# Attention's small operations moved from VectorE to GpSimd, its reciprocals moved behind the next group's minima, and an early root in the last stage

## The chip, the cores and the metric

The kernel runs on one core of a Trainium2 chip. A core has five engines with a queue of instructions each, which run in order: TensorE (PE in the profile, its weight loads PEld), VectorE (DVE), ScalarE (ACT), GpSimd (POOL) and SyncE (SP, which only issues DMAs here). The metric is the device time of one execution in microseconds, as the median of three runs: 1259.7 us (1258.15 to 1260.27).

## What is computed

One decoder layer over 1024 tokens of width 1024, in float32. Two branches read the same normalised input: a state-space branch and an attention branch with 16 heads of 64. Their outputs are gated, merged, projected and normalised. Of the reference, what the change touches is the softmax of the attention and the last norm:

```python
# attention, in blocks of 128 queries; fcum is a running sum of gates
s = einsum('bhqd,bhkd->bhqk', q[blk], k[:q1]) * scale
s = s + fcum[q0:q1, None] - fcum[None, :q1]
s = where(kpos <= qpos, s, -inf)
o[blk] = einsum('bhqk,bhkd->bhqd', softmax(s), v[:q1])
...
# end of the layer
out = einsum('bld,de->ble', merged, w_out)
x = x + out * rsqrt(mean(out * out) + eps) * post_g
```

## The kernel before, in words

**TensorE's work.** Nearly all time of TensorE goes into large projections. Each pair of output units is computed as seven half-size block products (a scheme that saves one product in eight), and each float32 operand is split into a high and a low part, so that one product is 12 matmuls of 128 x 128 x 512. `Pair` holds such a pair, `Stream` the fixed order of all its products, `halves(n)` issues the next n half products. Splits of operands (`wop` for weights at L366 and L367, `x0` to `x6` for activations at L273 to L279) lie on ScalarE (the high part, a copy) and on VectorE (the low part, a subtraction). Results leave PSUM by ScalarE (L426, L437) and VectorE (L439 to L443).

**The stages.** A prologue normalises the input; then the state-space branch, the attention (about 676 to 1108 us in the profile) and the last stages run, each with products of the stream between their own matmuls. The order on TensorE is written out by hand. On the other engines a scheduler places instructions, but those wrapped in `pin` keep their order among each other, and a `high_priority` block goes first.

**The attention.** Eight pairs of heads (`hp`), six groups each (`g`), 48 in all, counted by `m`. A group is two query blocks against one half of the keys:

```python
GROUPS = [((7, 4), 1), ((7, 4), 0), ((6, 5), 1), ((6, 5), 0), ((3, 0), 0), ((2, 1), 0)]
```

Blocks 7 and 4 (part 0) and 6 and 5 (part 1) take two groups, one for each half of the keys; blocks 3, 0, 2 and 1 (part 2) need only the lower half. So a part ends with each group of odd `g`; `end(m)` names it. In a round of the loop over `m`:

- `scores` issues the score matmuls into four PSUM tiles named `s`. Scores come out negated. For each of the four a VectorE instruction adds the gate sums `fb` and the mask and takes the row minimum `nm` (L1571, with a short read of the accumulator behind it), and ScalarE makes the exponential into `ex` with its row sum `sm` (L1575).
- `weighted` issues the matmuls of the group before, transposed weights `p` times values, into `av`. `free` (L1530) takes `av` out of PSUM.
- For a part that ends here, `settle` compares the minima of its two halves: `nr` is the smaller one (L1476), `dd` the difference of each to it (L1478, one instruction for each half), and ScalarE turns `dd` into exponentials (L1479).
- `masks` lets GpSimd write masks for later groups (L1437 into `fb`, L1446 into a part of `ex`).
- `stream.halves` issues projections.
- `scale` then forms the factors of the part: `sm` times `dd` (L1490), the sum over the two halves (L1492), its reciprocal (L1493), and `ns`, which is `dd` times one half times the reciprocal (L1495, twice). A part 2 has one half only: reciprocal (L1486) and half of it (L1487). All of it is on VectorE, on 4 or 8 columns.
- `turned` transposes the group's weights on TensorE into PSUM tiles that share their four buffers with `s`. ScalarE (L1614) and, for one block in four in the first six pairs, VectorE (L1612) copies them out to `p`; only then is the tile free for new scores. In the middle of the transposes of the group behind a part's end, TensorE transposes `ns` too; `send` and `take` bring it through DRAM into a broadcast form `rb`, and `out` multiplies by it (L1536, L1542, L1544).

GpSimd also issues the DMAs that store `ya_dram`, `ga_dram`, `ms_dram`, `t_s` and `t_a`; such an issue waits in GpSimd's queue for its data.

**The last stage.** `outcome(i)` takes row block `i` of the result in two halves `ch`: ScalarE squares the half and sums it into `ssq` (L1147), GpSimd multiplies by the norm's weights (L1150), and `finish` takes the square root on ScalarE (L1161), its reciprocal on VectorE (L1162) and writes the output (L1164). The square root needs another table in ScalarE than the exponentials and tanh before it; the load of it (ACT_TABLE_LOAD) stands in front of the first root.

Of the kernel before, what the change touches and what calls it, by code (L numbers as in the profile page):

```python
# [12 lines left out]
ALU = mybir.AluOpType  # L13
# [73 lines left out]
def hybrid_layer(ctx: ExitStack, tc, a, out):  # L87
# [43 lines left out]
    def pin(op):  # L131
        return tc.keep_in_program_order(op)

    def small(name="th"):
        return gp.tile([P, HALF], F32, tag="th", name=name)
# [995 lines left out]
    def outcome(i):  # L1131

        o, g, xr, st = {}, {}, {}, {}

        def begin(ch):
            xr[ch] = wp.tile([P, KH, P], F32, tag="raw", bufs=6, name="xr").rearrange("p a b -> p (a b)")
            nc.sync.dma_start(xr[ch], a["x"][i * P : (i + 1) * P, half(ch)])

        def dst(ch):
            o[ch] = fin["pool"].tile([P, HALF], F32, tag="ot", bufs=5, name="ot")  # L1140
            return o[ch]

        def post(ch):
            if not st:
                st["ssq"] = fin["pool"].tile([P, 2], F32, tag="ssq", bufs=4, name="ssq")
            ssq = st["ssq"]
            nc.scalar.activation(small("sq").bitcast(BF16)[:, 0:HALF], o[ch], AF.Square, accum_out=ssq[:, ch : ch + 1])  # L1147

            g[ch] = small("g") if i >= 6 else o[ch]
            (nc.vector if i >= 6 else nc.gpsimd).tensor_tensor(g[ch], o[ch], fin["postg"][:, half(ch)], ALU.mult)  # L1150
            if i == NT - 1:
                nc.vector.tensor_scalar(ssq[:, 1:2], ssq[:, 1:2], 1.0 / D, 4.0 * EPS, ALU.mult, ALU.add)
                return
            if len(o) < 2:
                return
            r = ssq[:, 0:1]
            nc.vector.tensor_tensor(r, r, ssq[:, 1:2], ALU.add)
            finish(r, eps4)

        def finish(r, bias):  # L1160
            nc.scalar.activation(r, r, AF.Sqrt, bias=bias, scale=1.0 / D)  # L1161
            nc.vector.reciprocal(r, r)  # L1162
            for c in range(2):
                nc.vector.scalar_tensor_tensor(o[c], g[c], r, xr[c], ALU.mult, ALU.add)  # L1164
                (nc.sync, nc.scalar)[c].dma_start(out[i * P : (i + 1) * P, half(c)], o[c])

        def direct(ch, ps):
            dst(ch)
            g[ch] = small("g")
            r = st["ssq"][:, 0:1]  # L1170
            with tc.high_priority():
                nc.scalar.activation(small("sq").bitcast(BF16)[:, 0:HALF], ps, AF.Square, accum_out=r)
                nc.vector.scalar_tensor_tensor(
                    g[ch], ps, -1.0, fin["postg"][:, half(ch)], ALU.mult, ALU.mult
                )
                finish(r, st["ssq"][:, 1:2])

        if i == NT - 1:
            post.direct = direct

        return dst, post, begin
# [214 lines left out]
    with tc.tile_pool(name="att", bufs=1, reuse_waits="tile", side="right") as ap, tc.tile_pool(  # L1396
# [55 lines left out]
        class Heads:  # L1452
# [16 lines left out]
            def settle(self, n):  # L1469

                if n == 2:
                    return
                nr = ap.tile([P, 2, 2], F32, tag="nr", name="nr")
                dd = self.dd[n] = ap.tile([P, 2, 2, 2], F32, tag="dd", name="dd")
                nm = self.nm[n]
                nc.vector.tensor_tensor(nr, nm[:, :, 0], nm[:, :, 1], ALU.min)  # L1476
                for h in range(2):
                    nc.vector.tensor_tensor(dd[:, :, h], nr, nm[:, :, h], ALU.subtract)  # L1478
                nc.scalar.activation(dd, dd, AF.Exp)  # L1479

            def scale(self, n):

                sm = self.sm[n]
                ns = self.ns[n] = ap.tile([P, 2, 2, 2], F32, tag="ns", name="ns")
                if n == 2:
                    nc.vector.reciprocal(sm, sm)  # L1486
                    nc.vector.tensor_scalar(ns, sm, 0.5, None, ALU.mult)  # L1487
                    return
                dd = self.dd[n]
                nc.vector.tensor_tensor(sm, sm, dd, ALU.mult)  # L1490
                total = sm[:, :, 0]
                nc.vector.tensor_tensor(total, total, sm[:, :, 1], ALU.add)  # L1492
                nc.vector.reciprocal(total, total)  # L1493
                for h in range(2):
                    nc.vector.scalar_tensor_tensor(ns[:, :, h], dd[:, :, h], 0.5, total, ALU.mult, ALU.mult)  # L1495

            def turn(self, n, tp):

# [228 lines left out]
        def end(m):  # L1727

            hp, g = divmod(m, 6)
            if 0 <= hp < NK and g % 2:  # L1730
                yield heads[hp], g // 2
# [29 lines left out]
        for m in range(6 * NK + 1):  # L1761

            if m < 6 * NK:
                hp, g = divmod(m, 6)
                if not g:
                    heads[hp] = Heads(hp)
                for u in range(2):
                    scores(hp, g, u)
            for one in made:
                weighted(*one)  # L1770
            for hd, which in end(m - 1):
                hd.free(which)
            if m == 6 * NK:
                stream.release()
                heads[NK - 1].out(2)
                break
            for hd, which in end(m - 2):
                if hd.last and which and m < 6 * NK - 1:
                    hd.out(which)
            for fn in deferred:  # L1780
                fn()
            deferred.clear()
            stream.release()
            for hd, which in end(m):
                hd.settle(which)
            masks(m)
            ahead, behind = room(m)
            stream.halves(ahead)

            for hd, which in end(m):  # L1790
                hd.scale(which)
                hd.load_gates(which)
            if m == 6 * NK - 1:
                heads[hp].out(1)
                for fn in deferred:
                    fn()
                deferred.clear()
            loads(m)
            made = turned(hp, g, list(end(m - 1)))
            if g in (1, 3):  # L1800
                masked(hp, {1: 5, 3: 0}[g])
            for hd, which in end(m - 2):
                if not hd.last or not which:
                    hd.out(which)
            if m == 6 * NK - 1:
                tp = pp.tile([P, HALF], F32, tag="s", bufs=4, name="tp")
                heads[hp].turn(2, tp)
                heads[hp].send(2, tp)
            if m % 6 == 0:
                for fn in later:  # L1810
                    fn()
                later.clear()
            stream.hold()
            stream.halves(behind)
            for hd, which in end(m if m == 6 * NK - 1 else m - 1):
                hd.take(which)
# [59 lines left out]
```

## Time and profile before

| | |
|---|---|
| median of three runs | 1259.7 us |
| lowest and highest | 1258.15, 1260.27 us |
| the profiled execution | 1260.92 us, its span 1259.2 us |
| granted TensorE clock over it | 0.998 |
| the attention, span time | about 676 to 1108 us |
| last matmul begins | 1252.5 us |

The span runs from the first to the last instruction of the program; 1.7 us of the execution lie outside it. The page gives busy time by engine. A busy TensorE is not one at its peak, since matmuls overlap and their ends are modelled; so a late matmul is found by its start. A line of the timeline has the start in us from the span's start, the length, engine, source line, operation, the tiles written and read, the shapes and a count, and in brackets the idle time of the engine before it with what ended it. The wait lists say which instruction waited for which, with the total, the count and the longest.

### The profile page before, as it was taken

How to read it: one execution, taken by the hardware profiler on the slowest of the kernel's cores; microseconds unless marked ns; L12 is line 12 of the kernel's file. 1: busy time of each engine (PE TensorE's matmuls, PEld its weight loads, DVE VectorE, ACT ScalarE, POOL GpSimd, SP SyncE). 2: the span in 40 equal slices, each digit the busy share in tenths (PEclk: the TensorE clock that was granted, in tenths of full speed). 3: DMA queues.
4: the chain of work that ended last, by engine and by line, in shares of the span. 5: the costliest groups of instructions: out<-in, count | busy, mean ns of one | idle time of the engine just before them, and what ended most of it. 6: DMA issues, size and time to landing. Idle time of an engine off the chain costs nothing.

```text
span 1259.2 us, 20989 instructions
## 1 busy us (share of the span) xinstructions
PE 1238.8 (98%) x6920; PEld 992.1 (79%) x6920; DVE 1011.6 (80%) x1979; ACT 789.1 (63%) x1736; POOL 337.3 (27%) x384
## 2 busy tenths in 40 slices
PE   7999999999999999999999999999999999999997
PEld 5688888888888888888888777777777777788886
DVE  7898886888788977998776677767799767997975
ACT  7745665556655766567555666666686667843753
POOL 3000440013301241015111334333122332366062
PEclk9999999999999999999999999999999999999999
DMA  8143442655347443744465476666787667766932
GB/s 305 55 126 92 143 157 93 201 151 188 120 129 212 165 124 115 229 147 140 147 207 195 156 246 220 225 208 196 258 296 266 201 197 254 266 206 214 355 119 99
DMA packets 162476, 233.57 MB, mean 185 GB/s; under 512 B 15200, under 2 KB 73024, under 8 KB 162368
## 3 DMA queue, kind: packets, MB, share of 16 engines
q1 hardware_dynamic: 140400, 196.22, 48.9%
q10 hardware_dynamic: 16464, 17.93, 4.0%
q0 software_dynamic: 5504, 18.09, 3.7%
q8 instruction: 54, 0.88, 0.3%
q14 instruction: 54, 0.44, 0.1%
HBM read 162.99 MB, written 72.34 MB: 187 GB/s over the span
## 4 chain that ended last, share of the span: by engine, by line
PE 85%; ACT 5%; DVE 4%; DMA 4%; issue 1%; SPq 0%; DVEq 0%; ACTq 0%; POOL 0%
PE pb L126 37%; PE pc L126 21%; PE pd L126 7%; PE av L126 5%; PE pt L129 5%; PE s L126 5%; PE yps L126 2%; PE st L126 1%; ACT wop L366 1%; DMA xr<-in_x 1%; PE tr L129 1%; PE tr_v L129 1%; PE df L126 1%; DMA csb<-cs_dram 1%; DMA xt<-in_x 1%
## 5 line engine op out<-in xcount | busy, mean ns | idle before, releaser
L366 ACT ACTIVATE wop<-sum 128x512 fp32r<-128x512 f32 x180 | 112.3, 626 | 103.7 <-DVE sum L372 46.0
L367 DVE TENSOR_TENSOR wop<-sum,wop 128x512 fp32r<-128x512 f32 x180 | 135.4, 753 | 50.4 <-ACT wop L366 49.2
L1575 ACT ACTIVATE ex<-ex,nm 128x512 f32<-128x512 f32 (+1 forms) x192 | 116.4, 608 | 71.2 <-DVE nm L1571 69.4
L426 ACT ACTIVATE s<-pb 128x512 f32<-128x512 f32 x143 | 84.7, 593 | 90.0 <-PE pb L126 87.5
L126 PE MATMUL pb<-x0h,wop 128*128 128x512 f32 x384 | 131.5, 398 | 0.0
L126 PE MATMUL pc<-x3h,wop 128*128 128x512 f32 x384 | 129.8, 396 | 0.7 <-DVE ot L443 0.4
L126 PE MATMUL pc<-x2h,wop 128*128 128x512 f32 x384 | 130.0, 397 | 0.0
L126 PE MATMUL pb<-x4h,wop 128*128 128x512 f32 x384 | 129.2, 395 | 0.0
L126 PE MATMUL pb<-x5h,wop 128*128 128x512 f32 x376 | 126.9, 395 | 0.7 <-ACT s L426 0.7
L126 PE MATMUL pb<-x6h,wop 128*128 128x512 f32 x376 | 126.7, 395 | 0.7 <-ACT s L426 0.7
L367 DVE TENSOR_TENSOR wop<-raw,wop 128x512 fp32r<-128x512 f32 x144 | 106.6, 740 | 20.5 <-ACT wop L366 20.4
L1571 DVE CUSTOM_DVE_ANT_0 ex<-s,fb 128x512 f32<-128x512 f32 (+1 forms) x128 | 79.1, 652 | 30.0 <-PE s L126 24.5
L366 ACT ACTIVATE wop<-raw 128x512 fp32r<-128x512 f32 x144 | 89.8, 624 | 19.5 <-PE pd L126 12.2
L126 PE MATMUL pd<-x1h,wop 128*128 128x512 f32 x288 | 95.8, 392 | 0.0
L126 PEld LDWEIGHTS pc<-x3h,wop 128*128 128x128 f32 x384 | 72.1, 188 | 18.5 <-issue 2.4
L210 POOL TENSOR_TENSOR wd<-wd 128x256 f32<-128x256 f32 x32 | 31.6, 986 | 204.2 <-DMA wd<-in_wo 126.6
L126 PEld LDWEIGHTS pb<-x4h,wop 128*128 128x128 f32 x384 | 72.1, 188 | 17.3 <-issue 2.5
L126 PEld LDWEIGHTS pc<-x2h,wop 128*128 128x128 f32 x384 | 72.1, 188 | 17.1 <-issue 2.0
L126 PEld LDWEIGHTS pb<-x0h,wop 128*128 128x128 f32 x384 | 72.2, 188 | 16.0 <-issue 1.5
L126 PEld LDWEIGHTS pb<-x5h,wop 128*128 128x128 f32 x376 | 70.7, 188 | 17.7 <-issue 1.8
L126 PEld LDWEIGHTS pb<-x6h,wop 128*128 128x128 f32 x376 | 70.6, 188 | 17.1 <-issue 1.6
L126 PE MATMUL pb<-x4l,wop 128*128 128x512 f32 x192 | 75.0, 390 | 0.4 <-DVE x4l L1254 0.4
(315 smaller groups left out, 3038.7 us busy)
## 6 DMA issues: line engine op xcount, KB each, us to landing
raw<-in_wu SPq DMA_DIRECT2D x128, 256.0 KB
csb<-cs_dram SPq DMA_DIRECT2D x32, 256.0 KB
q<-q_dram SPq DMA_DIRECT2D x32, 256.0 KB
k<-k_dram SPq DMA_DIRECT2D x16, 512.0 KB
fb<-f_dram SPq DMA_DIRECT2D x16, 512.0 KB
rb<-st_dram SPq DMA_DIRECT2D x48, 128.0 KB
wd<-in_wo SPq DMA_DIRECT2D x40, 128.0 KB
xt<-in_x SPq DMA_DIRECT2D x8, 512.0 KB
```

The lines of the kernel that those rows point to most:

```text
L126: return tc.keep_in_program_order(nc.tensor.matmul(*args, **kw))
L129: return tc.keep_in_program_order(nc.tensor.transpose(out_, in_, idn))
L210: pin(nc.gpsimd.tensor_tensor(t[out_], t[a_], t[b_], ALU.subtract))
L366: nc.scalar.activation(op[:, 0], src, AF.Copy)
L367: self.low = nc.vector.tensor_tensor(op[:, 1], src, op[:, 0], ALU.subtract).ins
L426: self.kept = nc.scalar.activation(s, ps, AF.Copy).ins
L1571: nc.vector.tensor_tensor_reduce(o, s[e][:, 0:w], f[:, e], 1.0, 3.0e38, ALU.add, ALU.min, nm)
L1575: pin(nc.scalar.activation(o, o, AF.Exp, scale=-1.0, bias=nm, accum_out=hd.at(hd.sm, i, h, e)))
```

## The change

Four things are done, all in the attention but the last.

1. The two differences of `settle` become one instruction over both halves.
2. In `scale`, the product with `dd`, the sum over the halves and a doubling (in place of the factor one half) go to GpSimd. A part 2 has nothing there any more.
3. The reciprocal stays on VectorE, but moves to a new `factors`, called in the next round behind the scores of the next group, so it stands pinned behind that group's four minima. The last product, `ns`, goes to GpSimd, pinned too. The very last part stays on VectorE and where it was.
4. In the last stage, behind the first half of row block 1 on ScalarE, a square root of a single column is taken and thrown away.

```diff
             ssq = st["ssq"]
+            if (i, ch) == (1, 0):
+                pin(nc.scalar.activation(warm, epst, AF.Sqrt))
             nc.scalar.activation(small("sq").bitcast(BF16)[:, 0:HALF], o[ch], AF.Square, accum_out=ssq[:, ch : ch + 1])
...
                 nc.vector.tensor_tensor(nr, nm[:, :, 0], nm[:, :, 1], ALU.min)
-                for h in range(2):
-                    nc.vector.tensor_tensor(dd[:, :, h], nr, nm[:, :, h], ALU.subtract)
+                nc.vector.tensor_tensor(dd, nr.unsqueeze(2).to_broadcast([P, 2, 2, 2]), nm, ALU.subtract)
                 nc.scalar.activation(dd, dd, AF.Exp)
 
             def scale(self, n):
+
+                if n == 2:
+                    return
+                sm, dd = self.sm[n], self.dd[n]
+                nc.gpsimd.tensor_tensor(sm, sm, dd, ALU.mult)
+                total = sm[:, :, 0]
+                nc.gpsimd.tensor_tensor(total, sm[:, :, 1], total, ALU.add)
+                nc.gpsimd.tensor_tensor(total, total, total, ALU.add)
+
+            def factors(self, n):
 
                 sm = self.sm[n]
                 ns = self.ns[n] = ap.tile([P, 2, 2, 2], F32, tag="ns", name="ns")
                 if n == 2:
-                    nc.vector.reciprocal(sm, sm)
-                    nc.vector.tensor_scalar(ns, sm, 0.5, None, ALU.mult)
+                    if self.last:
+                        with tc.high_priority():
+                            nc.vector.reciprocal(sm, sm)
+                            nc.vector.tensor_scalar(ns, sm, 0.5, None, ALU.mult)
+                        return
+                    pin(nc.vector.reciprocal(sm, sm))
+                    pin(nc.gpsimd.tensor_scalar(ns, sm, 0.5, None, ALU.mult))
                     return
-                dd = self.dd[n]
-                nc.vector.tensor_tensor(sm, sm, dd, ALU.mult)
                 total = sm[:, :, 0]
-                nc.vector.tensor_tensor(total, total, sm[:, :, 1], ALU.add)
-                nc.vector.reciprocal(total, total)
-                for h in range(2):
-                    nc.vector.scalar_tensor_tensor(ns[:, :, h], dd[:, :, h], 0.5, total, ALU.mult, ALU.mult)
+                pin(nc.vector.reciprocal(total, total))
+                total = total.unsqueeze(2).to_broadcast([P, 2, 2, 2])
+                pin(nc.gpsimd.tensor_tensor(ns, self.dd[n], total, ALU.mult))
...
                 for u in range(2):
                     scores(hp, g, u)
+                for hd, which in end(m - 1):
+                    hd.factors(which)
             for one in made:
...
                 hd.scale(which)
+                if m == 6 * NK - 1:
+                    hd.factors(which)
                 hd.load_gates(which)
```

The order of TensorE's instructions stays as it was; on SyncE two loads change places. Three places show what moves. Lines of the changed kernel lie 2 to 13 further down than the same line before.

VectorE at the end of part 0 of the sixth head pair (953 to 962 us in the profile before): `ISA` is a minimum or the read of its accumulator, `x2l` a split of the stream, `th` and `wop` products and splits of it. Before:

```order
L1476 TENSOR_TENSOR nr<-nm 128x4
L1478 TENSOR_TENSOR dd<-nr,nm 128x2x2 x2
L439 TENSOR_TENSOR th<-pc,s 128x512
L277 SCALAR_TENSOR_TENSOR x2l<-x2l,x2h 128x512 x2
L1105 SCALAR_TENSOR_TENSOR th<-th 128x512
L367 TENSOR_TENSOR wop<-raw,wop 128x512
L1490 TENSOR_TENSOR sm<-sm,dd 128x8
L1612 COPY p<-pt 128x512
L1536 TENSOR_TENSOR zr<-o,rb 128x512
L1492 TENSOR_TENSOR sm<-sm 128x2x2
```

The same place in the changed kernel:

```order
L1478 TENSOR_TENSOR nr<-nm 128x4
L1479 TENSOR_TENSOR dd<-nr,nm 128x8
L439 TENSOR_TENSOR th<-pc,s 128x512
L277 SCALAR_TENSOR_TENSOR x2l<-x2l,x2h 128x512 x2
L1105 SCALAR_TENSOR_TENSOR th<-th 128x512
L367 TENSOR_TENSOR wop<-raw,wop 128x512
L1625 COPY p<-pt 128x512
L1549 TENSOR_TENSOR zr<-o,rb 128x512
```

The product and the sum are gone from here; the reciprocal of this part now stands behind the four minima that follow, and ahead of the `av` product of that round.

GpSimd at the same place: `ex<-fb,far` are masks, DMA rows are issues. Before:

```order
L1437 TENSOR_TENSOR fb<-fb,far 128x128 x2
L192 DMA t_a<-x 128x512
L192 DMA t_a<-y 128x512
L1106 DMA ms_dram<-th 128x512
L1446 TENSOR_TENSOR ex<-fb,far 128x256 x2
L1645 DMA ya_dram<-zr 128x512
L192 DMA t_a<-x 128x512
```

The same place in the changed kernel:

```order
L1439 TENSOR_TENSOR fb<-fb,far 128x128 x2
L192 DMA t_a<-x 128x512
L192 DMA t_a<-y 128x512
L1487 TENSOR_TENSOR sm<-sm,dd 128x8
L1489 TENSOR_TENSOR sm<-sm 128x2x2
L1490 TENSOR_TENSOR sm<-sm 128x2x2
L1448 TENSOR_TENSOR ex<-fb,far 128x256 x2
L1106 DMA ms_dram<-th 128x512
L1658 DMA ya_dram<-zr 128x512
L1508 TENSOR_TENSOR ns<-dd,sm 128x8
L192 DMA t_a<-x 128x512
```

Three small operations and later the factor come in, and the issue of `ms_dram` now stands behind the two masks and no longer ahead of them.

ScalarE in the last stage, where row block 1 begins (`ot` is a half of the result, `sq` its square). Before:

```order
L437 ACTIVATE ot<-pb 128x512
L366 ACTIVATE wop<-sum 128x512
L1147 ACTIVATE sq,ssq<-ot 128x512
L1161 ACT_TABLE_LOAD
L1161 ACTIVATE ssq<-ssq,eps_72 128x1
L366 ACTIVATE wop<-merged 128x512
```

The same place in the changed kernel:

```order
L437 ACTIVATE ot<-pb 128x512
L1148 ACT_TABLE_LOAD
L1148 ACTIVATE warm<-epst 128x1
L366 ACTIVATE wop<-sum 128x512
L1149 ACTIVATE sq,ssq<-ot 128x512
L1163 ACTIVATE ssq<-ssq,eps_72 128x1
L366 ACTIVATE wop<-merged 128x512
```

The load of the table stands two instructions earlier, in front of a split and not in front of the root.

## The prediction

> **What bounds the kernel now.** I read the busy times first, then the busy time by stretches of 40 us, then what TensorE waited for, and last the order of time around each wait. The first line of the page, with busy time, share of the span and instructions of each engine:
>
> ```profile
> PE 1238.8 (98%) x6920; PEld 992.1 (79%) x6920; DVE 1011.6 (80%) x1979; ACT 789.1 (63%) x1736; POOL 337.3 (27%) x384
> ```
>
> TensorE (PE) is the bound. VectorE (DVE) is 20% idle, so time taken off it counts only where TensorE waits for it. The busy time by stretches gives busy us of PE, PEld, DVE, ACT and POOL, then the granted clock, the DMA share and GB/s:
>
> ```profile
> 920.00:960.00 40.00, 37.94 (x250) 28.51 (x250) 39.78 (x90) 33.10 (x83) 12.88 (x22) 1.00 0.91 320
> 956.80:960.10 3.30, 1.83 (x16) 1.24 (x16) 3.30 (x6) 0.44 (x1) 1.85 (x3) 1.00 0.85 295
> 960.20:963.50 3.30, 3.30 (x17) 1.63 (x14) 1.71 (x12) 2.81 (x9) 0.56 (x1) 0.50 0.66 167
> ```
>
> From 920 to 960 us DVE has next to no idle time (39.78 of 40) and PE loses 2.06 us, more than in any other stretch of the attention. Directly behind, PE runs at half its clock (0.50). The waits of PE, with total us, times and the longest:
>
> ```profile
> PE s L126 <- DVE p L1612: 1.5, 1, 1.5
> PE s L126 <- ACT p L1614: 0.4, 1, 0.4
> PE pc L126 <- DVE ot L443: 0.4, 1, 0.4
> ```
>
> The first is the largest wait of PE in the attention or behind it, the third stands in the last stage. The same places in order of time (start, length, instruction, idle time before it):
>
> ```profile
> 922.79 1.95 PE L126 MATMUL av<-p,v 128*64 128x256 f32 x16
> 939.94 0.82 PE L126 MATMUL s<-k,q 64*128 64x128 f32 x6 [0.39 <-ACT p L1614]
> 957.00 0.90 PE L126 MATMUL s<-k,q 64*128 64x384 f32 x7
> 959.36 0.62 PE L126 MATMUL s<-k,q 64*128 64x256 f32 x5 [1.47 <-DVE p L1612]
> 959.91 3.48 PE L126 MATMUL av<-p,v 128*64 128x256 f32 x16
> ```
>
> PE stands 1.47 us for a copy of transposed weights, and the next sixteen matmuls take 3.48 us where sixteen of the same shape took 1.95 at 922.79: 1.5 us more. Why the copy was late, on DVE:
>
> ```profile
> 956.43 0.69 DVE L367 TENSOR_TENSOR wop<-raw,wop 128x512 fp32r<-128x512 f32 x1
> 957.04 1.67 DVE L1490 TENSOR_TENSOR sm<-sm,dd 128x8 f32<-128x8 f32 x1
> 958.63 0.68 DVE L1612 COPY p<-pt 128x512 f32<-128x512 f32 x1
> ```
>
> And on GpSimd (POOL) at the same time:
>
> ```profile
> 956.81 0.54 POOL L1106 DMA_DIRECT2D ms_dram<-th  x1 [6.57 <-DVE th L1105]
> 957.37 1.30 POOL L1446 TENSOR_TENSOR ex<-fb,far 128x256 f32<-128x256 f32 x2
> ```
>
> The copy queued behind one of the very instructions that the change moves, a product of 8 columns that took 1.67 us while POOL worked at the side and ended with it.
>
> **The change part by part.** *What leaves DVE.* The groups of the attention (count, busy us, mean ns, idle before):
>
> ```profile
> L1478 DVE TENSOR_TENSOR dd<-nr,nm 128x4 f32<-128x4 f32 x32 | 4.7, 189 | 0.5
> L1495 DVE SCALAR_TENSOR_TENSOR ns<-dd,sm 128x4 f32<-128x4 f32 x32 | 4.7, 188 | 0.3
> L1490 DVE TENSOR_TENSOR sm<-sm,dd 128x8 f32<-128x8 f32 x16 | 4.2, 262 | 7.0 <-ACT dd L1479 6.9
> L1492 DVE TENSOR_TENSOR sm<-sm 128x4 f32<-128x4 f32 x16 | 2.6, 162 | 0.4
> L1487 DVE TENSOR_SCALAR ns<-sm 128x8 f32<-128x8 f32 x8 | 2.2, 274 | 0.2
> ```
>
> Gone are 4.7 + 4.2 + 2.6 of the three groups in the middle, 7 of 8 of the last (1.9), and of the 32 differences one of each two (2.3): some 15 us in all, and 6.9 us of standing for the exponential. The reciprocals stay and move behind the next minima. Nearly all of this is worth nothing: PE waits for DVE by 1.5 us in the 430 us of the attention, so that is what a lighter DVE can give back, and what hangs on it.
>
> *The place at 957 us.* Without the product the copy can start where the product did, 957.04 instead of 958.63: 1.6 us earlier. Other edits in the full stretch cancel, some 0.2 us each: one product and one difference leave, one reciprocal comes in. What can eat the gain is POOL. The change puts three small additions and products on it, then, ahead of the DMA issue that used to hold them back, the two mask additions. The nearest rows for what POOL and DVE do to each other, first DVE:
>
> ```profile
> 793.08 1.10 DVE L1476 TENSOR_TENSOR nr<-nm 128x4 f32<-128x4 f32 x1
> ...
> 925.98 2.02 DVE L277 SCALAR_TENSOR_TENSOR x4l<-x4l,x4h 128x512 fp32r<-128x512 f32 x2
> ```
>
> Then POOL, with the spread of its narrowest operation last:
>
> ```profile
> 792.86 1.30 POOL L210 TENSOR_TENSOR x<-x,th 128x512 f32<-128x512 f32 x1 [7.76 <-DMA x<-ys_dram]
> ...
> 925.29 1.32 POOL L1446 TENSOR_TENSOR ex<-fb,far 128x256 f32<-128x256 f32 x2
> 926.57 1.72 POOL L1437 TENSOR_TENSOR fb<-fb,far 128x128 f32<-128x128 f32 x2
> L1437 POOL TENSOR_TENSOR fb<-fb,far x64: 420/432/977, 660.6 to 1089.0; 128x128 f32<-128x128 f32 x64
> ```
>
> At 793 a 4-column minimum stands until POOL's 1.30 us are over. At 926 two operations of each side take turns: POOL needs 1.72 us for what takes twice 0.43 alone. So in this kernel a DVE instruction on two SBUF tensors and a POOL one do not run together. [...]
>
> A small POOL operation is in no row. Below it is bounded by the 0.16 us that DVE needs for 4 columns (L1492), above by the 0.43 of 128 columns; I take 0.16, since the many times wider one costs only 0.43. Three of them ahead of the copy take 0.5 us from DVE, and the two mask additions 1.3 more if they too get in ahead. The copy then comes 1.6 us earlier (nothing in the way), 1.1 (the three small ones, by turns as at 926), or 0.2 later (all five first, as the product at 957 stood through both masks). I take 1.1, because the turns at 926 are the case with DVE work of the same size waiting.
>
> *The clock.* A wait of 1.47 − 1.1 = 0.4 us stays. The row at 939.94 has 0.39, and the stretch that holds it was granted 1.00. So I expect no half clock, and back come the 3.4 us at half speed: 1.7 us (1.5 by the two rows of sixteen matmuls, the rest on the matmul behind them). [...]
>
> *Reciprocals behind the next minima.* They no longer stand at the head of DVE's queue for sums that are not there. What is late next is the chain to the transposes of the factors on PE. The tightest of the 23, the last minimum on DVE:
>
> ```profile
> 1000.12 0.08 DVE L1571 DVE_READ_ACCUMULATOR2_ANT nm<- 128x1 f32 x1
> ```
>
> And PE:
>
> ```profile
> 1001.76 0.27 PE L129 MATMUL pt<-ident,ns 128*8 128x128 f32 x1
> ```
>
> From 1000.20 there are 1.56 us. A reciprocal (0.2), at most one DVE operation that holds POOL off (0.7) and the factor on POOL (0.16 to 0.43) end after 1.1 to 1.3 us. It fits, so nothing. POOL's masks come up to 2 us later, since they queue behind a factor that waits for the reciprocal; the minima that read them are a group, some 9 us, on.
>
> *The root of one column.* ScalarE (ACT) in the last stage:
>
> ```profile
> 1199.93 0.64 ACT L366 ACTIVATE wop<-sum 128x512 fp32r<-128x512 f32 x1 [1.47 <-DVE sum L372]
> 1201.19 1.28 ACT L1161 ACT_TABLE_LOAD   x1
> 1202.49 0.30 ACT L1161 ACTIVATE ssq<-ssq,eps 128x1 f32<-128x1 f32 x1
> ```
>
> DVE and then PE beside it:
>
> ```profile
> 1202.82 0.16 DVE L1162 RECIPROCAL ssq<-ssq 128x1 f32<-128x1 f32 x1 [1.45 <-ACT ssq L1161]
> 1202.89 0.67 DVE L443 TENSOR_TENSOR ot<-s,pc 128x512 f32<-128x512 f32 x1
> ...
> 1202.87 0.39 PE L126 MATMUL pb<-x4h,wop 128*128 128x512 f32 x1
> 1203.62 0.50 PE L126 MATMUL pc<-x3h,wop 128*128 128x512 f32 x1 [0.36 <-DVE ot L443]
> ```
>
> The 1.28 us load and a 0.30 root need 1.6 us and go into a gap of 1.47, so the next split starts 0.1 late at most. The square root, the reciprocal and the subtraction behind them come 1.2 us earlier. PE's matmuls of this size start 0.23 us apart; here it was 0.75, so 0.5 us of PE come back. Afterwards PE has work without a gap until the tail.
>
> Sum: 1.1 + 1.7 + 0.5 = 3.3 us. The profiled execution took 1260.92 us, which gives 1257.6. It lies 1.2 above the median of 1259.7, so the forecast for the median is 1256.4. A difference of 0.2%, 2.5 us, is about what a measurement of this kernel can tell from none; the runs of before spread over 2.1 us.
>
> **The rivals.** *POOL goes first.* [...] For it speaks the 1.67 us product, which stood through both masks; against it the turns at 926.
>
> *The clock falls anyway.* [...] Then 1.1 + 0.5 = 1.6, 1258.1. Against it: the half clock begins within 1 us of the wait's end, and nowhere else in the attention.
>
> *The factors come late.* [...] PE then stands at the transposes of the factors. By the same reading as at 1001.76 the seven third parts, the tightest, have margins of 1.6 to 3.3 us from the last minimum. At 3.0 us from minimum to factor, where this decides, they lose 3.8 us together, and the place at 957 gives nothing, since its three small operations cost as much: 1259.7 − 0.5 + 3.8 = 1263.0. For it speaks that no small POOL operation is in the trace; against it the 0.43 us of the wider one.
>
> **How the numbers follow.** The forecast has 0.47, the clock 0.18, POOL first 0.24, late factors 0.11. Faster by over 0.2% (below 1257.2) is the forecast and a sliver of the clock's case: 0.48. Slower is the last rival: 0.11. The same takes 0.41. The range reaches down to 1.6 + 1.7 + 0.5 and the 0.4 at 939.94, 4.2, and half the spread of the runs, 1.1: 1254.4. Up it takes POOL first with 0.8 of spread: 1260.2. The forecast's own range is 1255 to 1257.6.
>
> **What would show it.** Right: PE's list has no wait of over 0.6 us for a DVE copy, no stretch at 0.50 near 960, PE busy over 39.0 in the stretch from 920, no wait for ot in the last stage, and a table load that ends about when ACT's sum split can start. Wrong: a 128x8 operation on POOL over 0.5 us in the median, PE waiting at the transposes of ns, or the same 3 us given back at another full stretch of DVE.

## The result and the profile after

The changed kernel takes 1257.01 us in the median of 22 runs (1255.80 to 1258.01), the kernel before 1258.89 in as many runs beside them (1257.57 to 1262.59). The medians differ by 1.9 us. The ratio over the runs is 0.9983, with a 95% interval of 0.9976 to 0.9989: 2.1 us faster, between 1.4 and 3.0. The profiled execution of the changed kernel took 1256.17 us with a span of 1254.5, so the two profiled executions (1260.92 and 1256.17 us) are 4.75 us apart, more than twice what the medians differ by. Where the rest comes from is half of this study.

The busy line and the stretch from 920 us of the changed kernel, and of its list of what PE waits for the copies of p:

```profile
PE 1236.3 (99%) x6920; PEld 991.0 (79%) x6920; DVE 1003.6 (80%) x1892; ACT 789.4 (63%) x1737; POOL 358.9 (29%) x455
```

```profile
920.00:960.00 40.00, 39.03 (x262) 29.05 (x261) 39.50 (x93) 33.69 (x86) 15.35 (x27) 1.00 0.89 313
```

```profile
PE s L126 <- DVE p L1625: 0.4, 1, 0.4
...
PE s L126 <- ACT p L1627: 0.4, 1, 0.4
```

DVE is 8 us lighter, POOL 22 us heavier, and DVE is as full from 920 to 960 as it was (39.50 of 40). The wait of 1.5 us for p is gone, the wait for ot too. The 0.4 for a DVE copy of p is a wait at another place, 930.25, and a new one: neither profile of the kernel before has it. The place at 957 in the changed kernel, PE, then DVE, then POOL:

```profile
956.33 1.33 PE L126 MATMUL s<-k,q 64*128 64x384 f32 x12
957.59 1.95 PE L126 MATMUL av<-p,v 128*64 128x256 f32 x16
959.46 0.50 PE L126 MATMUL pb<-x5h,wop 128*128 128x512 f32 x1
```

```profile
953.88 1.29 DVE L277 SCALAR_TENSOR_TENSOR x2l<-x2l,x2h 128x512 fp32r<-128x512 f32 x2
955.09 0.68 DVE L1105 SCALAR_TENSOR_TENSOR th<-th 128x512 f32<-128x512 f32 x1
955.70 0.68 DVE L367 TENSOR_TENSOR wop<-raw,wop 128x512 fp32r<-128x512 f32 x1
956.30 0.68 DVE L1625 COPY p<-pt 128x512 f32<-128x512 f32 x1
```

```profile
954.15 0.48 POOL L1487 TENSOR_TENSOR sm<-sm,dd 128x8 f32<-128x8 f32 x1 [4.60 <-ACT dd L1480]
954.70 0.53 POOL L1489 TENSOR_TENSOR sm<-sm 128x4 f32<-128x4 f32 x1
955.31 0.52 POOL L1490 TENSOR_TENSOR sm<-sm 128x4 f32<-128x4 f32 x1
955.79 1.76 POOL L1448 TENSOR_TENSOR ex<-fb,far 128x256 f32<-128x256 f32 x2
```

The twelve score matmuls run through without a stop, and the sixteen behind them take 1.95 us at a granted clock of 1.00 (the stretch from 957.80 to 961.10). DVE's operations up to the copy keep their usual 0.6 to 0.7 us, one behind the other; it is the three small POOL operations that take 0.5 us each here. The masks still make DVE stand, but only the operation behind the copy (zr<-o,rb took 1.20 us, before 0.68), and PE does not wait for that one. The usual price of the small POOL operations is in the groups (minimum, median and maximum in ns):

```profile
L1487 POOL TENSOR_TENSOR sm<-sm,dd x16: 192/202/692, 687.3 to 1076.8; 128x8 f32<-128x8 f32 x16
L1508 POOL TENSOR_TENSOR ns<-dd,sm x16: 191/200/552, 696.4 to 1085.1; 128x8 f32<-128x8 f32 x16
L1503 POOL TENSOR_SCALAR ns<-sm x7: 227/228/452, 732.4 to 1047.0; 128x8 f32<-128x8 f32 x7
```

The last stage, ACT first, then PE:

```profile
1194.39 1.28 ACT L1148 ACT_TABLE_LOAD   x1
...
1195.96 0.63 ACT L366 ACTIVATE wop<-sum 128x512 fp32r<-128x512 f32 x1
...
1197.43 0.29 ACT L1163 ACTIVATE ssq<-ssq,eps 128x1 f32<-128x1 f32 x1 [0.23 <-DVE ssq L1159]
```

```profile
1198.78 0.39 PE L126 MATMUL pb<-x4h,wop 128*128 128x512 f32 x1
1199.01 0.39 PE L126 MATMUL pc<-x3h,wop 128*128 128x512 f32 x1
```

The load now stands where ACT had its gap of 1.47 us, the root takes 0.29 instead of standing behind 1.28, and the two matmuls are 0.23 us apart, where they were 0.75.

One number says most about each kernel below. From the first of the twelve score matmuls at that place to the matmul behind the sixteen products there are 28 matmuls in the same order in every kernel. In the kernel before they go from 957.00 to 963.32, 6.32 us; in the changed kernel from 956.33 to 959.46, 3.13. I call it the stretch of 28. The second number is the gap between the two matmuls of the last stage, 0.75 or 0.23.

### The profile page after: what moved, and what is told of

It reads as the page before. It is cut to its first block, busy times and chain, and to the rows that moved or that the text cites. A ratio compares the mean times of both kernels' runs of the same rounds, so it can differ in the third digit from the quotient of the medians.

```text
span 1254.5 us, 20953 instructions
## 1 busy us (share of the span) xinstructions
PE 1236.3 (99%) x6920; PEld 991.0 (79%) x6920; DVE 1003.6 (80%) x1892; ACT 789.4 (63%) x1737; POOL 358.9 (29%) x455
## 4 chain that ended last, share of the span: by engine, by line
PE 89%; ACT 4%; DVE 3%; DMA 3%; issue 1%; SPq 0%; DVEq 0%; ACTq 0%
PE pb L126 39%; PE pc L126 22%; PE pd L126 7%; PE av L126 5%; PE pt L129 5%; PE s L126 5%; PE yps L126 2%; PE st L126 1%; PE tr L129 1%; PE tr_v L129 1%; ACT wop L366 1%; PE df L126 1%; PE pv L126 1%; PE tr L126 0%; DMA raw<-in_wv 0%
## 5 line engine op out<-in xcount | busy, mean ns | idle before, releaser
L912 POOL TENSOR_TENSOR xe<-xdt,tend 128x256 f32<-128x256 f32 x28 | 26.2, 937 | 175.3 <-DVE xdt L875 170.3
```

What stands on the lines that cost most here:

```text
L912: nc.gpsimd.tensor_tensor(xe, s["xdt"], tend[:, c, hs].unsqueeze(2).to_broadcast([P, 4, 64]), ALU.mult)
```

## The experiments

Each was timed in five rounds beside the kernel before, on one of three chips. So medians of different rows do not compare as they stand: the kernel before took 1258.89 us beside the changed kernel, 1259.83 beside e1 to e4, 1260.26 beside e5 to e8 and 1260.17 beside e9 to e12. The intervals of most ratios are some 0.0009 to 0.0010 (1.2 us) to either side, so single ratios decide little between theories that differ by 1 us; the stretch of 28 and the gap are exact to some 0.05 us, but are those of one execution.

| kernel | median, us | ratio, 95% interval | stretch of 28, us | gap, us |
|---|---|---|---|---|
| before, first profile | | | 6.32 | 0.75 |
| changed | 1257.01 | 0.9983, 0.9976 to 0.9989 | 3.13 | 0.23 |
| e1 before again | 1259.85 | 1.0001, 0.9992 to 1.0010 | 4.79 | 0.75 |
| e2 root only | 1259.61 | 0.9994, 0.9985 to 1.0003 | 4.79 | 0.23 |
| e3 attention only | 1259.21 | 0.9989, 0.9979 to 0.9999 | 3.13 | 0.75 |
| e4 one place | 1258.94 | 0.9991, 0.9982 to 1.0000 | 3.22 | 0.74 |
| e5 masks behind copy | 1258.67 | 0.9986, 0.9977 to 0.9995 | 3.27 | 0.75 |
| e6 reciprocals in front | 1257.64 | 0.9978, 0.9970 to 0.9987 | 3.13 | 0.23 |
| e7 copy twice | 1258.52 | 0.9988, 0.9980 to 0.9997 | 3.89 | 0.23 |
| e8 copy three times | 1259.12 | 0.9991, 0.9982 to 1.0000 | 4.45 | 0.23 |
| e9 masks twice | 1263.36 | 1.0025, 1.0014 to 1.0037 | 7.64 | 0.74 |
| e10 small operations flood | 1275.68 | 1.0121, 1.0102 to 1.0141 | 3.16 | 0.23 |
| e11 masks behind copy, root | 1258.30 | 0.9984, 0.9973 to 0.9994 | 3.28 | 0.23 |
| e12 product behind copy | 1257.71 | 0.9979, 0.9969 to 0.9990 | 2.96 | 0.23 |

**The kernel before, again.** No edit.

> The kernel before, unchanged, profiled a second time and timed against itself. The profile of before showed a wait of 1.47 us for the copy of transposed weights at 957 us and 3.4 us at a granted clock of 0.50 behind it; against it the changed kernel gained 1.79 us in the wait and 1.5 us in the clock, 4.75 us over the whole span, while the medians of 22 runs each differ by 1.9. Theory A (the place is there in every execution, the half clock only in some, so that the first profile was an unlucky one): this profile shows a wait of 1.2 to 1.6 us at the same matmul and a granted clock near 1.00 behind it, and a span of about 1257. Rival B (wait and half clock are there every time, and the changed kernel gives something back in most executions): again 1.5 us and 0.50, span about 1259. Rival C (the wait itself comes and goes): under 0.6 us. Timed against itself: ratio 1.000.

The matmul at the place and the stretch that was at half clock in the first profile, in this second one:

```profile
959.35 0.62 PE L126 MATMUL s<-k,q 64*128 64x256 f32 x5 [1.47 <-DVE p L1612]
959.90 1.95 PE L126 MATMUL av<-p,v 128*64 128x256 f32 x16
```

```profile
960.20:963.50 3.30, 3.30 (x24) 2.26 (x21) 3.23 (x14) 2.85 (x10) 0.56 (x2) 1.00 0.50 154
```

The wait is there to the hundredth, 1.47 us, and the clock stays at 1.00. That is theory A: the wait is there again, the half clock is not. The span of 1257.7 is nearer to A's 1257 than to B's 1259.

**The early root alone.** The two lines of the change that stand in the last stage, in the kernel before.

```diff
+            if (i, ch) == (1, 0):
+                pin(nc.scalar.activation(warm, epst, AF.Sqrt))
```

> The kernel before with the early root alone. Theory: TensorE loses its 0.5 us wait for ot in the last stage, the ratio is 0.9996, 0.5 us faster; the wait at 957 us stays as it was. Rival (the table load of 1.28 us only moves and delays the splits behind it): 0.0 to +0.5 us, and a wait of TensorE of some 0.3 us for a weight split near 1199 us.

The gap falls from 0.75 to 0.23, so 0.52 us of PE come back, and no weight split delays PE instead. The ratio's middle, 0.9994, is 0.75 us; its interval includes none. The stretch of 28 is 4.79, wait and full clock, which makes the third profile with that wait and the second without a half clock.

**The attention's part alone.** The changed kernel without those two lines.

> The changed kernel without the early root, so the attention's part alone. Theory: it carries what is left of the 1.9 us between the medians, 1.4 us (ratio 0.9989), no wait for the copy near 957 us over 0.6 us and no half clock; TensorE waits 0.5 us for ot in the last stage as in the kernel before. Rival (the last stage carries most, the attention nothing): ratio 0.9998 or more.

The forecast of 0.9989 was met, and the stretch of 28 is the changed kernel's. The gap is back at 0.75. The span of this profile is 1259.5, above the kernel before's second one: PE waits 1.67 us for one matmul of an early stage, at 234.85 us, that the change does not touch. The mean granted clock of this execution is 0.999, as in the profiles of e1 and e2.

**One place.** Of the 16 groups of products only the one at 957 goes to GpSimd.

```diff
+        PLACE = (5, 0)
...
+                if (self.hp, n) == PLACE:
+                    sm, dd = self.sm[n], self.dd[n]
+                    nc.gpsimd.tensor_tensor(sm, sm, dd, ALU.mult)
...
```

> The kernel before with one of the attention's 16 groups of products changed, the one whose product took 1.67 us ahead of the copy at 957 us: its product, sum and doubling go to GpSimd, its reciprocal behind the next minima, its factors to GpSimd; its differences and all other groups stay on VectorE. Theory (the whole gain of the attention comes from this place): the same time as the attention's part alone, within 0.4 us, and a wait at 957 us under 0.6 us. Rival (the lighter VectorE of all 48 groups is what helps): at most a third of that gain, under 0.5 us.

The stretch of 28 is 3.22, 0.09 above the whole change, and the ratios are 0.9991 and 0.9989, each to some 0.001. The other 15 groups add no gain that can be seen.

**The masks behind the copy.** Nothing moves off VectorE. One column of p is copied on GpSimd ahead of the two mask additions, so that they can start only when the copy of p is done. If the two additions are why the product took 1.67 us, it takes 0.2 here, the copy comes 1.5 us earlier and PE's wait for it falls under 0.4 us.

```diff
             w = (i % 4 + 1) * P
+            if (hp, i) == (5, 5):
+                pin(nc.gpsimd.tensor_copy(seen, copies[31][:, 0, 1, 0:1]))
             for e in range(2):
```

> The kernel before with one more GpSimd instruction, a copy of one column of p, ahead of the two mask additions that ran beside the product of 1.67 us at 957 us. It reads the copy of transposed weights, so both mask additions start behind that copy; VectorE's order is that of before, word for word, and the product stays ahead of the copy. [...] Rival (the product was late or slow for its own inputs, or VectorE's queue is simply full there): product and wait as before, ratio 1.000.

DVE in this kernel, then POOL:

```profile
958.48 0.16 DVE L1494 TENSOR_TENSOR sm<-sm,dd 128x8 f32<-128x8 f32 x1
958.56 0.69 DVE L1617 COPY p<-pt 128x512 f32<-128x512 f32 x1
```

```profile
958.26 0.54 POOL L1106 DMA_DIRECT2D ms_dram<-th  x1 [6.57 <-DVE th L1105]
959.31 0.60 POOL L1448 COPY seen<-p 128x1 f32<-128x1 f32 x1 [0.51 <-PE s L126]
959.88 1.30 POOL L1450 TENSOR_TENSOR ex<-fb,far 128x256 f32<-128x256 f32 x2
```

The same product in the same place of the same queue, beside the same DMA issue, takes 0.16 us instead of 1.67, with both additions behind the copy. The mask additions were what held it. The wait at the place is gone, and the ratio of 0.9986 cannot be told from the 0.9989 of the attention's part.

**Reciprocals in front again.** The changed kernel with each reciprocal and factor product right behind its sum.

```diff
-                for hd, which in end(m - 1):
-                    hd.factors(which)
...
-                if m == 6 * NK - 1:
-                    hd.factors(which)
+                hd.factors(which)
```

> The changed kernel with each reciprocal and factor product right behind its sum again, so the reciprocals stand on VectorE ahead of the next group's minima; GpSimd keeps the small operations. Theory (VectorE then stands for sums that GpSimd has not finished, some 0.1 to 0.8 us each, and little of it reaches TensorE, which has slack in most groups): idle time of VectorE ahead of the 23 reciprocals 3 to 8 us in all against under 1 in the changed kernel, and a time 0.0 to 0.5 us above the changed kernel's (ratio 0.9983 to 0.9987). Rival (the move of the reciprocals is what carries the gain, since a standing VectorE delays its copies): at least 1 us back, ratio 0.9991 or more, with waits of TensorE for DVE p.

The group of the reciprocals, with the idle time of DVE ahead of them at the end:

```profile
L1506 DVE RECIPROCAL sm<-sm 128x4 f32<-128x4 f32 x16 | 2.8, 174 | 7.1 <-POOL sm L1490 7.0
```

DVE stands 7.0 us for GpSimd's sums, as the theory had it, and PE loses nothing by it: the stretch of 28 is 3.13 and the ratio 0.9978, if anything below the changed kernel's. Moving the reciprocals saves DVE 7 us that nobody waits for.

It even costs something, at 930 us. PE there in the changed kernel, with DVE and POOL ahead of it:

```profile
930.25 1.14 PE L126 MATMUL s<-k,q 64*128 64x384 f32 x11 [0.45 <-DVE p L1625]
```

```profile
926.99 2.03 DVE L279 TENSOR_TENSOR x1l<-x1l,x1h 128x512 fp32r<-128x512 f32 x2
928.95 0.92 DVE L367 TENSOR_TENSOR wop<-sum,wop 128x512 fp32r<-128x512 f32 x1
```

```profile
927.60 1.72 POOL L1439 TENSOR_TENSOR fb<-fb,far 128x128 f32<-128x128 f32 x2
```

The same operations with the reciprocals in front again:

```profile
928.71 1.28 DVE L279 TENSOR_TENSOR x1l<-x1l,x1h 128x512 fp32r<-128x512 f32 x2
929.91 0.68 DVE L367 TENSOR_TENSOR wop<-sum,wop 128x512 fp32r<-128x512 f32 x1
```

```profile
926.76 1.71 POOL L1439 TENSOR_TENSOR fb<-fb,far 128x128 f32<-128x128 f32 x2
```

In the changed kernel POOL waits for the reciprocal before the factor, so the masks behind the factor come later, by some 1.5 us. They now run beside DVE's splits x1l and wop (2.03 and 0.92 us instead of 1.28 and 0.68), and the copy of p stands behind these. The wait of 0.45 us is in the profiles of the changed kernel, e3, e7, e8 and e12; before, e1, e2, e4, e5, e6 and e11 have none there.

**The copy made twice, and three times.** The changed kernel with the copy of p at that place repeated (the edit for two copies; for three, `range(2 ...)`).

```diff
-                        nc.vector.tensor_copy(to, src)
+                        copies.append(p)
+                        one = nc.vector.tensor_copy(to, src)
+                        if len(copies) == 32:
+                            pin(one)
+                        for _ in range(1 if len(copies) == 32 else 0):
+                            pin(nc.vector.tensor_copy(to, src))
```

> The changed kernel with the copy of transposed weights at the place near 957 us made twice, and TensorE waits for the second; VectorE's order is the same otherwise. Its wait of 0.4 us there becomes 1.0. Theory (the clock falls behind a wait of about 1.5 us, in some executions): 0.6 us slower than the changed kernel, granted clock 1.00 behind the wait. Rival (any wait that is longer than the harmless 0.4 of the trace can halve the clock): 0.50 for some 3.4 us behind it, 2.3 us slower in the profile.

> The same with three copies; the third stands behind two of the next minima on VectorE, so the wait becomes about 0.4 + 2 x 0.6 + 2 x 0.6 = 2.8 us. Theory (the longer wait makes the fall of the clock the rule): 0.50 for 3.4 us or so behind it and 2.4 + 1.7 = 4.1 us slower than the changed kernel. [...]

Both expectations started from a wait of 0.4 that is not at this place (it is at 930.25). With two copies the wait is 0.57 and the stretch of 28 grows by 0.76; the ratio moves by 0.0005, as 0.6 us would. With three, PE's next score matmul does not wait for the third copy but for a minimum that comes before it, 1.02 us, and the stretch grows by 1.32, not 2.4. The clock is 1.00 in both. So waits of 0.57 and 1.02 us left the clock alone here, and the question of the longer wait was left to the next kernel.

**The masks made twice.** The kernel before, with the two mask additions that ran beside the product made over again.

```diff
-            for e in range(2):
+            for e in (0, 1, 0, 1) if (hp, i) == (5, 5) else (0, 1):
```

> The kernel before with the two mask additions that ran beside the product at 957 us made twice over, with the same operands, four in a row on GpSimd. VectorE's order up to the copy is that of before. Theory (the product stands until GpSimd's row of operations is over): the product takes 1.67 + 2 x 0.65 = 3.0 us, TensorE's wait there becomes 2.8 us instead of 1.5, the ratio 1.0010, and behind so long a wait the half clock comes in the profile too, 1.5 us more for such an execution. Rival (after two operations of GpSimd the turn goes to VectorE): product 1.7, wait 1.5, ratio 1.000.

DVE, POOL and PE at the place, and PE's clock (the column behind the busy times) by pieces of it:

```profile
959.02 2.91 DVE L1490 TENSOR_TENSOR sm<-sm,dd 128x8 f32<-128x8 f32 x1
```

```profile
958.80 0.54 POOL L1106 DMA_DIRECT2D ms_dram<-th  x1 [6.57 <-DVE th L1105]
959.35 2.54 POOL L1446 TENSOR_TENSOR ex<-fb,far 128x256 f32<-128x256 f32 x4
```

```profile
962.58 0.89 PE L126 MATMUL s<-k,q 64*128 64x256 f32 x5 [2.71 <-DVE p L1612]
963.40 3.29 PE L126 MATMUL av<-p,v 128*64 128x256 f32 x16
```

```profile
959.90:962.50 2.60, 0.00 (x0) 0.00 (x0) 2.60 (x3) 0.00 (x0) 1.99 (x4) 1.00 0.62 203
962.60:963.40 0.80, 0.80 (x5) 0.57 (x6) 0.80 (x3) 0.00 (x0) 0.00 (x0) 0.59 0.00 0
963.40:966.60 3.20, 3.20 (x17) 1.69 (x16) 1.81 (x11) 2.81 (x9) 0.56 (x1) 0.57 0.37 107
966.60:970.00 3.40, 3.40 (x19) 2.83 (x18) 3.03 (x5) 1.12 (x2) 0.54 (x1) 1.00 0.91 320
```

The product of 8 columns stands until the fourth addition is over: 2.91 us, against an expected 3.0. PE waits 2.71, and the clock drops. The time is 3.2 us above the kernel before: 1.2 for the longer wait, and the rest for the most part the half clock (1.5 to 1.7), which the kernel before mostly does not have. The mean clock of each of the twelve executions bears this out: eight have 0.996 to 0.998 and took 1264.3 us on average, four have 0.999 and took 1261.6. So the fall is frequent behind this wait, but not in every execution. The rival, by which the turn goes to DVE after two operations, is out.

**Small operations by the dozen.** The changed kernel with eight more products of 128x8 on GpSimd ahead of each of the 23 factor products.

```diff
...
+                for _ in range(8):
+                    pin(nc.gpsimd.tensor_tensor(spare, self.dd[n], total, ALU.mult))
                 pin(nc.gpsimd.tensor_tensor(ns, self.dd[n], total, ALU.mult))
```

> The changed kernel with eight more small GpSimd products (128x8, into a tile that nobody reads) ahead of each of the 23 factor products, so the factors come later by 8 x 0.20 to 0.28 = 1.6 to 2.2 us. In the changed kernel's trace the 23 factor products on GpSimd end 1.03 to 3.85 us before the transposes that read them; at 1.9 us of delay four of them are late, by 0.9, 0.75, 0.5 and 0.4 us. Theory (late factors were a real limit, only too far off): 2.5 us slower than the changed kernel, ratio 1.0003, with waits of TensorE at ns. [...] Rival 2 (something else covers the factors): under 0.5 us.

What PE waits for, then the first such row on POOL in two pieces, and DVE beside it:

```profile
PE pt L129 <- POOL ns L1506: 8.3, 5, 3.1
PE pt L129 <- POOL ns L1513: 5.0, 5, 1.9
```

```profile
698.58 1.61 POOL L1512 TENSOR_TENSOR spare<-dd,sm 128x8 f32<-128x8 f32 x6 [3.01 <-DVE sm L1509]
...
700.27 1.38 POOL L1512 TENSOR_TENSOR spare<-dd,sm 128x8 f32<-128x8 f32 x2
701.62 0.20 POOL L1513 TENSOR_TENSOR ns<-dd,sm 128x8 f32<-128x8 f32 x1
```

```profile
698.41 0.66 DVE L1548 TENSOR_TENSOR o<-av,zr 128x512 f32<-128x512 f32 x1
699.51 0.69 DVE L441 TENSOR_TENSOR th<-pc,s 128x512 f32<-128x512 f32 x1 [0.44 <-PE pc L126]
700.17 0.69 DVE L367 TENSOR_TENSOR wop<-sum,wop 128x512 fp32r<-128x512 f32 x1
700.90 0.69 DVE L388 TENSOR_TENSOR sum<-sum,raw 128x512 f32<-128x512 f32 x1
```

The kind of loss was the theory's, the size was far off: 1.0121, some 17 us above the changed kernel, where 2.5 were expected. Six of the eight operations took 1.61 us, as expected, but the two that met wop<-sum,wop and sum<-sum,raw, which read SBUF alone, took 1.38. The eight took 3.07 us in all, not 1.6 to 2.2, and PE waits for ten factors instead of four, 13.3 us together. DVE's operations beside them keep their 0.66 to 0.69 us.

One thing more is in this profile. The longest of these waits and the granted clock behind it:

```profile
1012.73 0.27 PE L129 MATMUL pt<-ident,ns 128*8 128x128 f32 x1 [3.05 <-POOL ns L1506]
```

```profile
1012.70:1016.10 3.40, 3.37 (x21) 2.34 (x21) 0.56 (x1) 1.54 (x5) 1.83 (x4) 1.00 0.42 151
```

Behind 3.05 us of waiting the clock stays at 1.00, and so it does behind 1.50, 1.88 and 2.28 us in the same profile, whose mean clock is 1.000. The other four executions of this kernel have a mean clock of 0.996 and took 1.8 to 5.8 us more than the profiled one. So in these profiles the length of a wait alone does not tell whether the clock falls.

**The two places without the change.** The kernel before with the masks behind the copy and with the early root; no small operation moves, no reciprocal.

> The kernel before with the masks behind the copy at the one place and with the early root, and nothing else of the change: no small operation moves to GpSimd, no reciprocal moves. Theory (the whole gain of the change is these two places): the changed kernel's time, ratio 0.9980 to 0.9984. Rival (the lighter VectorE of the other groups gives part of it): 0.9988 or more.

Ratio 0.9984, stretch 3.28, gap 0.23: the changed kernel's gain to within some 0.001, with one column copied and one root moved.

**A product behind the copy.** The changed kernel with the 128x512 product th<-th (0.68 us on DVE) behind the copy of p instead of ahead of it.

```diff
+                        copies.append(p)
+                        if len(copies) == 32:
+                            pin(nc.vector.tensor_copy(to, src))
+                            pin(waiting[0]())
...
```

> The changed kernel with one product of the stream (th<-th, 128x512, 0.68 us on VectorE) put behind the copy of transposed weights near 957 us instead of ahead of it, the wait that is left there being 0.4 us. Theory: the copy comes 0.6 us earlier, TensorE's last wait for DVE p at that place goes, 0.4 us faster than the changed kernel, ratio 0.9980. Rival (the next wait in line, ScalarE's copies of p beside it, ends as late): 0.9983, unchanged.

The premise was wrong again, for the 0.4 it meant to remove is at 930.25. The stretch of 28 falls by 0.17 us to 2.96, and the ratio of 0.9979 cannot be told from the changed kernel's. None of the versions that were run is clearly faster than the changed kernel.

## Why the prediction was right, and where it was not

The forecast was 1256.4 us; the median came out at 1257.0, within the range. That it came so near is in part luck. The kernel before took 1259.7 us in the three runs that the forecast started from and 1258.89 beside the changed kernel, so the gain is 1.9 us by the medians and 2.1 by the ratio, against 3.3 forecast. And of its terms, the wait was put too low and the clock too high. The gain of 0.17% is just under the 0.2% that was set as the bound of no change, though 22 runs a side tell it from none.

**The place at 957.** The mechanism is the one that was read from the trace: the copy queued behind a small product that waited for GpSimd's mask additions. The experiments on the masks show it from both sides, without them 0.16 us, with twice as many 2.91. The term was sized at 1.1 us, with 1.6 as its upper end and 0.2 later as its lower one. The upper end came true: PE's stretch loses the whole 1.47 us wait. The step that failed is "Three of them ahead of the copy take 0.5 us from DVE". They take nothing from it: POOL's three operations took 0.48, 0.53 and 0.52 us while DVE's beside them kept 0.65 to 0.68. So no wait of 0.4 stayed at this place; the 0.4 that PE still loses for a DVE copy is the new one at 930.25.

**The clock.** "Back come the 3.4 us at half speed: 1.7 us" was right for the profiled execution: the stretch of 28 fell from 6.32 to 3.13 us there, 1.66 of it for the wait (4.79 to 3.13 by the profiles with the wait alone) and 1.53 for the clock (6.32 to 4.79), with 0.1 more on the matmul behind. It was wrong for the median. The step that failed is the last of the sum, by which the profiled execution lies 1.2 above the median and all terms carry over: the half clock was in one of three profiles with that wait. The mean clocks of all executions on record say how often it comes: of 120 with that wait (before, e1, e2) 37 have 0.998 or less, of 113 in which the wait at this place is at most 1.02 us (changed, e3 to e8, e11, e12) 13 have; the mean also counts the clock behind the last matmul, which is 0.50 from 1257.1 us to the end in the first profile of the kernel before and from 1250.5 in the changed kernel's. The averages of the two groups, 0.9987 and 0.9990, differ by about a fifth of what one half-clock stretch takes off (1.7 us of 1258, or 0.0014), so by this estimate it comes in one execution of five and is worth some 0.3 us on average. The wait, the clock, the gap of the last stage and the new wait at 930.25 then make 1.66 + 0.3 + 0.52 − 0.45 = 2.0 us, and 1.9 to 2.1 were measured. One profile could not have told this; a second one of the kernel before does.

**The rival on the clock**, 1.6 us less for the median, came nearer to the measured 2.1 than the forecast's 3.3. From the one profiled execution to the other the clock did come back where the wait was gone, from 0.50 (960.20 to 963.50 before) to 1.00 (957.80 to 961.10 in the changed kernel), but most executions had nothing to bring back. In the kernel with the masks made twice 2.71 us of waiting is followed by a half clock, and eight of twelve executions have a mean clock of 0.998 or less. That a wait need not be followed by one is shown by the flood, with 1.00 behind 3.05 us.

**The reciprocals** were put at nothing, and what they save is nothing: in front again they make DVE stand 7.0 us, and PE none. But the step "POOL's masks come up to 2 us later" was followed only to the minima that read the masks. The later masks also met two splits ahead of a copy, and PE lost 0.45 us at 930.25, a cost that is in no term of the sum. The intervals of the medians are too wide to show it.

**The small operations** were taken at 0.16 us and took 0.19 to 0.23 at their shortest. The factors end 1.03 us or more ahead of PE in the changed kernel, so the rival of late factors had no place to start; the flood shows that it would have been dear with the factors some 3 us later. DVE's busy time fell by 8 us, not by the 15 that were counted; no term of the sum hung on that.

**The early root** was put at 0.5 us and is 0.52, in every profile with it. The load fits the gap as worked out: the sum split behind it starts 0.13 us later than before by the same count (1195.96 against 1199.93 less the 4.1 us by which ACT runs ahead there).

**The rest of the 4.75 us between the two profiles**, some 0.9, is at other places: 0.67 is gained before 957 (with the loss at 930.25 taken off), 0.3 of it ahead of the attention, and 0.4 at a matmul near 1189 us that waits for ScalarE. In the second profile of the kernel before the early stages stand 0.9 us the other way, and with the early root alone the 0.5 at 1189 are gained ahead of that root. So this is how executions differ.

## What to carry to other kernels

Look for small VectorE instructions on SBUF tensors that stand in front of something TensorE waits for, and see what GpSimd does in the same microsecond: two mask additions held behind a copy, with the early root, gave, as far as can be told, what the whole change gave with its 71 more operations on GpSimd. The wait at 957 was in all three profiles of kernels that keep its cause, but other waits, such as 1.67 us at 235 us, came in one profile and not in others, and so did the half clock behind a wait; profile the kernel before twice before a term is carried to the median. And of a rearrangement, only what the bound engine waits for counts: 7 us of standing on VectorE were worth nothing, while masks that came some 1.5 us later cost 0.45.

## What the runs showed of the hardware

GpSimd and VectorE did not take turns evenly at 957 us. Beside an unbroken row of GpSimd's additions of 0.64 to 0.65 us each, a VectorE product of 8 columns ended only with the last one: 1.67 us with two of them (before), 2.91 with four (e9), and 0.16 where both stood behind the copy (e5). The product's record starts 0.33 us before the first addition's (959.02 against 959.35 in e9), and it stood through four of them all the same. It is not always so: near 926 us in the profile before, two splits of 512 columns took 2.02 us (1.28 at 954.63) beside GpSimd's additions of 128 columns, two of which took 1.72 (0.43 each in the median), so both sides lost. What decides between the two was not found. Beside VectorE's row of 0.65 to 0.68 us operations in the changed kernel, three small GpSimd operations took 0.48, 0.53 and 0.52 us (0.19 to 0.20 at their shortest), with no visible cost for VectorE. In the flood, at 698 us, six small GpSimd operations took 1.61 us (0.27 each) beside o<-av and th<-pc, which read PSUM; two took 1.38 (0.69 each) beside wop<-sum and sum<-sum, which do not; and the one behind these took 0.20.

The granted clock stayed at 1.00 behind waits of 0.57 (e7) and 1.02 us (e8). It fell to 0.50 in one of three profiles with 1.47 (before, but neither e1 nor e2), for 3.41 us from 960.16 to 963.57, and it fell in the one with 2.71 (e9, 0.59 and 0.57 over the two stretches from 962.60 to 966.60). In the flood it stayed at 1.00 behind 1.50, 1.88, 2.28 and 3.05 us. What decides, also between the three executions with the same wait, was not found.
